# Two-layer hybrid decoder trunk on one core: the sums of the seven-product output projection move to VectorE, the planner's port rule changes, and the second layer's weight sums start earlier

## The chip, the cores and the metric

The kernel runs on one core of one Trainium2 chip. The metric is the device time of one execution in microseconds (us). The kernel before took 1146.99 us in the median of three runs (1146.76 to 1147.99). The execution that the profiler recorded took 1147.56 us; its instructions span 1145.8 us of that, so 1.8 us lie around the span. TensorE's granted clock was 0.996 of full speed over that span.

## The reference

Two layers follow each other; each maps x (1024 tokens of 1024 floats) to a new x. Cut to what matters:

```python
h = rmsnorm(x, g_pre) @ w_in                       # 1024 x 3488
(a_q, a_k, a_v, b_b, b_c, b_x, c_q, c_kv, c_kr, d_q, d_k, d_v, gate) = split(h)
ya = sliding-window attention with sinks           # group A, 256 columns
yb = b_b * (conv3(b_c * b_x) + conv_b)             # group B, 256 columns
yc = low-rank latent attention, causal             # group C, 256 columns
yd = stick-breaking attention, strictly causal     # group D, 256 columns
y = rmsnorm per group(ya, yb, yc, yd) * silu(gate) # 1024 x 1024
x = x + rmsnorm(y @ w_out, g_post)                 # y @ w_out: 1024 x 1024 x 1024
```

All of it is float32. The kernel keeps the operands of its large products as two parts, a high part and the rest ("hi" and "lo"), and forms each product as hi*hi + hi*lo + lo*hi. Such a pair of parts is called a split here: ScalarE writes hi (a cast), VectorE or GpSimd writes lo (source minus hi).

## The kernel before

**Stages of a layer.** First come the norm of the rows of x and their transposes (`prenorm_rows`, `prenorm_cols`), then the projections in the order of the stream `gemm()`: the columns of group C (`c_cols`, "projection one", which ends with the mark `("cn", l, 7)`), group B, then D, the gates and A. Attention scores (`scores`), the products with the values (`pvs`) and the group norms (`norms`) run between them. The last stage is y @ w_out.

**The seven products.** y and w_out are cut into two by two blocks of 512, and y @ w_out is formed with seven block products in place of eight (a Strassen-Winograd scheme). Product m (1 to 7) needs a left operand, a block or a sum of blocks of y (`left`, `y_sums1`, `y_sums2`, `difference`), and a right operand, a block or a sum of blocks of w_out. The right operands don't depend on x. The stream `weight_sums` forms them beforehand: for each of four row pairs k, `w_sums` loads two rows of blocks of w_out into two "P" tiles, and for each of the seven m forms a sum where there is one (four of the seven m), splits it (ScalarE casts hi, VectorE or GpSimd subtracts) and writes the split to DRAM scratch `rd[m][k]`. So each k has 4 sums and 7 splits, 11 VectorE-or-GpSimd instructions of 128x512; there are four k in each of two layers, 88 instructions in all. The stream `operands` later loads them again (`right`).

**The end of a layer.** The stream `outs` runs the products in the order 1, 7, 6, 4, 5, 2, 3, each for four token tiles i, combines them on VectorE, and calls `squares` (ScalarE squares with a row sum; VectorE scales; for the second half GpSimd takes the power -0.5). A gain multiplication by `norm_post` follows: for the first 512 columns in `outs`, for the second in `out_tile` (GpSimd in both places, except for the very last tile). `out_tile` then adds the normalised tile to x with two VectorE instructions, and in layer one starts the next layer's norm for that tile.

**What sets the order.** The class `Weaver` keeps a clock of its own for each engine (`busy`), with an estimated length for each instruction (`enter`). `place` looks for the first free spot of an engine; for instructions that read two SBUF operands or otherwise use the port that VectorE and GpSimd share (`pair`), it also looks at the other engine's list `port`. The planned time becomes the instruction's priority, and `behind` pins the order along each engine. TensorE's instructions stand in the order in which the streams issue them: `run` always advances the stream whose next step is ready first. `sooner` picks the engine, VectorE or GpSimd, on which one instruction would end first by that clock. Nothing of this clock runs on the chip; it only fixes which engine an instruction goes to and the order of each engine's queue. Six P tiles are shared by scores, norms and weight sums, counted in `ptiles`; "g" tiles (34) hold operands and "W" tiles (3) hold projection weights.

All VectorE, ScalarE and GpSimd instructions carry the line L85 in the profile, since `Tracked` issues them; matmuls are L513, transposes L517, DMA issues L430. So groups are told apart by the names of their tiles: xP are P tiles (rows of w_out, scores, rows of x), xg operand tiles, xw weight tiles or PSUM banks of projections, xraw raw weights, xtr, xsc and xpv other PSUM banks, xt scratch, xss the row sums of the output norm, xrd the DRAM scratch of the right operands.

## Time and profile before

| | |
|---|---|
| median of three runs | 1146.99 us |
| profiled execution | 1147.56 us |
| its span | 1145.8 us |
| TensorE (PE) busy | 1111.4 us, 97% |
| VectorE (DVE) busy | 853.6 us, 75% |
| ScalarE (ACT) busy | 683.4 us, 60% |
| GpSimd (POOL) busy | 437.4 us, 38% |
| DMA | 141.19 MB, mean 123 GB/s |

TensorE is busy nearly all the time, so what can be won is the time in which it waits, and the ends of the program, where it does not run. Those waits stand in a few stretches; the views by stretches and the timelines of single engines show them. In a timeline a line is one instruction or a run of equal ones: start, duration, engine, source line, operation, output<-inputs, count, and in brackets the idle time of the engine before it with what ended that. An instruction's duration covers its write at the end; the next one of the same engine starts somewhat before that, so the distance from start to start is a little shorter than the duration.

### The profile page before, as it was taken

What the parts mean: (1) busy time and instruction counts of PE and PEld (TensorE: products, weight loads), DVE (VectorE), ACT (ScalarE), POOL (GpSimd) and SP (SyncE); (2) the same over time, 40 slices, a digit from 0 to 9 for tenths busy, and PEclk for the clock granted to TensorE, in tenths of its full rate; (3) what the DMA queues carried; (4) which work ended last, traced back from release to release, by engine and by line L of the source; (5) the groups of instructions that cost most, each with busy time, mean ns of one, the idle gap of its engine ahead of it and who ended that gap; (6) DMA issues with size and microseconds to landing.
All of it is one profiled execution on the core that took longest, in us unless ns stands there. A gap on an engine that the chain in (4) does not pass through costs nothing.

```text
span 1145.8 us, 18194 instructions
## 1 busy us (share of the span) xinstructions
PE 1111.4 (97%) x6206; PEld 960.8 (84%) x6206; DVE 853.6 (75%) x1695; ACT 683.4 (60%) x1505; POOL 437.4 (38%) x542
## 2 busy tenths in 40 slices
PE   8999999899999999999989999999999999999996
PEld 6988888888888888788779888889888888887885
DVE  6868689868778758946785586898788885788376
ACT  7666567447767558634764655664677774773332
POOL 3216155423364216611631341453453631364034
PEclk9999999999999999999999999999999999999998
DMA  6120304842352023356550212068413411136544
GB/s 222 46 65 29 84 19 135 332 140 93 102 193 74 19 56 138 130 202 216 184 160 19 65 45 58 19 216 298 160 64 123 162 56 37 38 138 243 199 184 165
DMA packets 89887, 141.19 MB, mean 123 GB/s; under 512 B 12426, under 2 KB 61896, under 8 KB 89796
## 3 DMA queue, kind: packets, MB, share of 16 engines
q1 hardware_dynamic: 89796, 140.04, 37.0%
q8 instruction: 49, 0.80, 0.3%
q14 instruction: 42, 0.34, 0.1%
HBM read 88.64 MB, written 45.09 MB: 117 GB/s over the span
## 4 chain that ended last, share of the span: by engine, by line
PE 79%; DVE 9%; ACT 5%; issue 3%; POOL 3%; DMA 1%; SPq 0%; POOLq 0%; DVEq 0%; ACTq 0%
PE xw L513 47%; PE xsc L513 13%; PE xtr L517 9%; PE xpv L513 7%; DVE xg L85 4%; PE xtr L513 3%; ACT xP L85 3%; DVE xP L85 2%; ACT xg L85 1%; POOL xs L85 1%; DVE xPT L85 1%; DVE xs L85 1%; POOL xg L85 1%; DVE xt L85 0%; ACT xt L85 0%
## 5 line engine op out<-in xcount | busy, mean ns | idle before, releaser
L513 PE MATMUL xw<-xg,xw 128*128 128x512 f32 x2064 | 514.4, 396 | 1.4 <-DVE xg L85 1.4
L513 PEld LDWEIGHTS xw<-xg,xw 128*128 128x128 f32 x2064 | 377.0, 188 | 75.6 <-PE xsc L513 1.6
L513 PE MATMUL xsc<-xg,xg 128*128 128x512 f32 (+6 forms) x992 | 207.2, 350 | 1.0 <-issue 1.0
L513 PEld LDWEIGHTS xsc<-xg,xg 128*128 128x128 f32 (+1 forms) x992 | 161.0, 189 | 17.8 <-issue 1.4
L513 PE MATMUL xw<-xg,xg 128*128 128x256 f32 (+2 forms) x792 | 155.5, 343 | 0.9 <-DVE xg L85 0.9
L85 POOL TENSOR_SCALAR xP<-xP,xs 128x256 f32<-128x256 f32 (+7 forms) x128 | 80.2, 638 | 158.4 <-DVE xs L85 84.7
L513 PEld LDWEIGHTS xw<-xg,xg 128*128 128x128 f32 x792 | 130.2, 191 | 12.0 <-DVE xg L85 1.6
L517 PE MATMUL xtr<-ident,xP 128*128 128x128 f32 (+1 forms) x843 | 121.5, 273 | 7.6 <-DVE xg L85 5.7
L85 ACT CAST xPT<-xtr 128x512 fp32r<-128x512 f32 (+1 forms) x192 | 101.2, 558 | 45.8 <-PE xtr L517 44.3
L85 DVE TENSOR_TENSOR xPT<-xtr,xPT 128x512 fp32r<-128x512 f32 (+1 forms) x192 | 116.2, 628 | 14.3 <-ACT xPT L85 13.8
L513 PE MATMUL xpv<-xPT,xg 128*128 128x256 f32 (+1 forms) x720 | 115.8, 287 | 1.7 <-DVE xg L85 1.3
L513 PEld LDWEIGHTS xpv<-xPT,xg 128*128 128x128 f32 x720 | 103.2, 189 | 12.9 <-DVE xg L85 2.6
L517 PEld LDWEIGHTS xtr<-ident,xP 128*128 128x128 f32 (+1 forms) x843 | 96.9, 140 | 17.6 <-issue 9.9
L85 ACT ACTIVATE xP<-xP,xs 128x256 f32<-128x256 f32 (+7 forms) x132 | 85.0, 646 | 42.4 <-DVE xs L85 34.6
L85 DVE TENSOR_TENSOR_SCAN xP<-xP,xP 128x128 f32<-128x128 f32 (+3 forms) x64 | 90.7, 1427 | 13.6 <-ACT xP L85 12.7
L85 POOL TENSOR_TENSOR xw<-xraw,xw 128x512 fp32r<-128x512 f32 (+1 forms) x37 | 51.0, 1378 | 120.5 <-ACT xw L85 86.3
L85 DVE TENSOR_TENSOR xg<-xw,xg 64x512 fp32r<-64x512 f32 (+1 forms) x94 | 64.7, 688 | 36.9 <-ACT xg L85 33.1
L85 POOL TENSOR_TENSOR xg<-xg,xg 128x512 f32<-128x512 f32 (+1 forms) x33 | 44.5, 1355 | 118.5 <-ACT xt L85 100.0
L85 DVE TENSOR_TENSOR xg<-xg,xg 128x512 fp32r<-128x512 f32 (+3 forms) x80 | 63.0, 817 | 28.2 <-ACT xg L85 22.9
L85 ACT ACTIVATE xP<-xsc 128x512 f32<-128x512 f32 (+2 forms) x192 | 80.3, 517 | 2.9 <-PE xsc L513 2.4
L85 POOL TENSOR_TENSOR xs<-xs,mhalf 128x1 f32<-128x1 f32 (+2 forms) x36 | 35.9, 997 | 106.8 <-DVE xs L85 106.8
L85 ACT ACTIVATE xt<-xg 128x512 f32<-128x512 f32 (+1 forms) x88 | 46.4, 539 | 46.6 <-DVE xg L85 36.5
(137 smaller groups left out, 1519.8 us busy)
## 6 DMA issues: line engine op xcount, KB each, us to landing
xrd<-xg SPq DMA_DIRECT2D x56, 512.0 KB, 3.8
xg<-xrd SPq DMA_DIRECT2D x56, 512.0 KB, 5.3
xraw<-in_w_in_dram SPq DMA_DIRECT2D x96, 256.0 KB, 2.9
xP<-in_w_out_dram SPq DMA_DIRECT2D x16, 512.0 KB, 5.1
xg<-xyd SPq DMA_DIRECT2D x12, 512.0 KB, 4.2
xg<-in_x_dram SPq DMA_DIRECT2D x8, 512.0 KB, 9.6
xg<-xP SPq DMA_DIRECT2D x32, 128.0 KB, 2.3
xyd<-xg SPq DMA_DIRECT2D x8, 512.0 KB, 3.0
```

Source lines behind the costliest of these rows:

```text
L85: ins = real(*args, **kw)
L513: in_order(T.matmul(ps, lhs, rhs, start=start, stop=stop, skip_group_check=True))
L517: in_order(T.transpose(ps, src, idn))
```

## The change

Five things change.

1. `place`: the search for a spot now moves an instruction behind every entry of the other engine's port list that overlaps it (`s < t + dur and e > t`). Before, it moved it only where its start lay inside such an entry (`s <= t < e`).
2. `w_sums`: the sums and the splits are all VectorE instructions; `sooner` is not asked. 
3. `difference`, and the gain multiplications in `outs` and `out_tile`, are VectorE instructions.
4. `weight_sums` of the second layer may start when layer one's `outs` has started (`("u", l - 1)`), unless its rows are already being made ready (`calm`). Until projection one of its layer has ended, its splits go to a W tile, afterwards to a g tile. The first layer's waits only for `("cn", 0, 7)`. Both ask that VectorE be free within 900 ns by the clock (700 before).
5. In the list of streams `weight_sums` stands ahead of `outs`.

The matmuls are the same in number and shape. GpSimd loses 88 instructions (547 to 459 in its queue) and VectorE gains 88 (1697 to 1785). Of these a few are splits of projection weights (`w_split`), which `sooner` now gives to the other engine; two of them, of 128x416, stood in GpSimd's queue between the powers of the first row norms, in the program's first 20 us, and are VectorE's now.

```diff
@@ place
-            end = max([e for s, e in other if s <= t < e], default=t)
+            end = max([e for s, e in other if s < t + dur and e > t], default=t)
@@ w_sums
-            yield lambda: W.room("g", 1, 34) and not W.room("W", 1, 3) and max(0.0, free() - 700.0, W.ready("A", rows) - 1000.0)
+            early = lambda: ("cn", L["l"], 7) not in W.done
+
+            def where():
+                if early():
+                    return "W" if W.room("W", 1, 3) else None
+                return "g" if W.room("g", 1, 34) and not W.room("W", 1, 3) else None
+
+            yield lambda: bool(where()) and max(0.0, free() - 900.0, W.ready("A", rows) - 1000.0)
+            spot = where()
             if x1 is not None:
-                W.sooner((G, V), 512, x1, x2).tensor_tensor(dst, x1, x2, ALU.add)
-            t = gtile([P, 2, 512])
+                V.tensor_tensor(dst, x1, x2, ALU.add)
+            t = wtile() if spot == "W" else gtile([P, 2, 512])
             A.copy(t[:, 0, :], dst)
-            W.sooner((G, V), 512, dst, t).tensor_tensor(
-                t[:, 1, :], dst, f(t[:, 0, :]), ALU.subtract
-            )
+            V.tensor_tensor(t[:, 1, :], dst, f(t[:, 0, :]), ALU.subtract)
@@ difference
-        W.sooner((V, G), 512, x1, x2).tensor_tensor(dst, x1, x2, ALU.subtract)
+        V.tensor_tensor(dst, x1, x2, ALU.subtract)
@@ out_tile
-        (V if L["last"] and t == NT - 1 else G).tensor_tensor(u1, z, L["gpost"][:, 512:1024], ALU.mult)
+        V.tensor_tensor(u1, z, L["gpost"][:, 512:1024], ALU.mult)
@@ outs, twice
-                G.tensor_tensor(u21[i], u21[i], gain[:, 0:512], ALU.mult)
+                V.tensor_tensor(u21[i], u21[i], gain[:, 0:512], ALU.mult)
@@ weight_sums
-            yield need(("xt", l, 7), ("cn", l, 7))
+            yield need(("u", l - 1) if l else ("cn", l, 7))
             free = W.idle_from("V")
+
+            def calm():
+                rows = l and ("right", l - 1, 5, 0) in W.done and ("B", l) not in W.done
+                return not rows and ptiles[0] >= 3 and max(0.0, free() - 900.0)
+
             for k in range(4):
-                yield lambda: ptiles[0] >= 3 and max(0.0, free() - 700.0)
+                yield calm
```

**Place 1, GpSimd's queue in layer one, between two group norms.** Here xt and xg_1794 are the value products' last additions, xP_2528 and xP_2529 the two rows of w_out of `w_sums`, xw with xraw a split of projection weights, xs with mhalf the power of a group norm. Before:

```order
L85 TENSOR_TENSOR xt_2500<-xt_2500 64x128
L85 TENSOR_TENSOR xg_1794<-xt_2500 64x128
L85 TENSOR_TENSOR xP_2528<-xP_2528 128x512
L85 TENSOR_TENSOR xw_2557<-xraw_2403,xw_2557 128x512
L85 TENSOR_TENSOR xP_2528<-xP_2529,xP_2528 128x512
L85 TENSOR_TENSOR xs_2624<-xs_2624,mhalf 128x4
```

Of the change:

```order
L85 TENSOR_TENSOR xt_2500<-xt_2500 64x128
L85 TENSOR_TENSOR xg_1794<-xt_2500 64x128
L85 TENSOR_TENSOR xw_2552<-xraw_2403,xw_2552 128x512
L85 TENSOR_TENSOR xs_2632<-xs_2632,mhalf 128x4
L85 TENSOR_TENSOR xt_2643<-xt_2643 64x128
```

The two weight sums are gone from this queue; they now stand in VectorE's.

**Place 2, VectorE's queue at the boundary of the layers, between the additions of product 5 (from banks xsc and xpv) and the first one of product 2 (from a bank xw).** Additions from a bank set it free for TensorE. xP_59xx and xP_60xx with xss are the additions to x, xP_5889 and xP_5890 rows of w_out of the second layer. Before:

```order
L85 TENSOR_TENSOR xg_5882<-xsc_6155,xg_5882 128x512
L85 TENSOR_SCALAR xs_6116<-xs_6116 128x1
L85 SCALAR_TENSOR_TENSOR xP_5997<-xg_5959,xss_198,xP_5997 128x512
L85 SCALAR_TENSOR_TENSOR xP_5997<-xt_6138,xss_198,xP_5997 128x512
L85 TENSOR_TENSOR xg_5882<-xpv_6186,xg_5882 128x512
L85 TENSOR_SCALAR xs_6147<-xs_6147 128x1
L85 TENSOR_SCALAR xss_198<-xss_198 128x1
L85 TENSOR_TENSOR xg_5729<-xw_6248,xg_5729 128x512
```

Of the change:

```order
L85 SCALAR_TENSOR_TENSOR xP_6054<-xt_6195,xss_198,xP_6054 128x512
L85 TENSOR_TENSOR xg_5922<-xsc_6210,xg_5922 128x512
L85 TENSOR_TENSOR xg_5922<-xpv_6224,xg_5922 128x512
L85 TENSOR_TENSOR xw_6303<-xP_5889,xw_6303 128x512
L85 TENSOR_TENSOR xP_5889<-xP_5890,xP_5889 128x512
L85 TENSOR_TENSOR xg_5729<-xw_6256,xg_5729 128x512
L85 TENSOR_TENSOR xP_5890<-xP_5889,xP_5890 128x512
L85 TENSOR_SCALAR xss_198<-xss_198 128x1
L85 TENSOR_TENSOR xg_5729<-xg_5729,xg_5726 128x512
L85 TENSOR_TENSOR xg_5729<-xw_6274,xg_5729 128x512
```

The last two tiles of product 5 are added later, a split and a sum of the second layer's weights stand ahead of product 2's first addition, and a gain multiplication (by xg_5726) stands between its first and second.

**Place 3, VectorE's queue at the end of the program, product 3's tiles two and three.** Before:

```order
L85 TENSOR_TENSOR xg_11768<-xsc_12155,xg_11768 128x512
L85 TENSOR_SCALAR xss_231<-xss_231 128x1
L85 TENSOR_TENSOR xg_11769<-xsc_12180,xg_11769 128x512
L85 SCALAR_TENSOR_TENSOR xP_12228<-xg_11766,xss_231,xP_12228 128x512
L85 SCALAR_TENSOR_TENSOR xP_12228<-xt_12339,xss_231,xP_12228 128x512
L85 TENSOR_SCALAR xss_231<-xss_231 128x1
```

Of the change:

```order
L85 TENSOR_TENSOR xg_11768<-xsc_12155,xg_11768 128x512
L85 TENSOR_TENSOR xt_12339<-xg_11768,xg_11763 128x512
L85 TENSOR_SCALAR xss_231<-xss_231 128x1
L85 SCALAR_TENSOR_TENSOR xP_12228<-xg_11766,xss_231,xP_12228 128x512
L85 SCALAR_TENSOR_TENSOR xP_12228<-xt_12339,xss_231,xP_12228 128x512
L85 TENSOR_TENSOR xg_11769<-xsc_12180,xg_11769 128x512
L85 TENSOR_TENSOR xt_12363<-xg_11769,xg_11763 128x512
```

The gain multiplication (xt<-xg) joined the queue, and the third tile's addition from its bank moved behind the second tile's two additions to x.

Where the second layer's 28 splits are written out, by their place among TensorE's 6206 matmuls: before, 21 between the 4178th and the 4579th and 7 between the 4907th and the 4978th; now 13 between the 2783rd and the 3072nd (during layer one's seven products, which run from the 2775th to the 3126th), one at the 3500th, and 14 between the 4199th and the 4526th. One pair of P tiles stays with `w_sums` from the 2707th to the 3500th.

## Rows read from the trace of the kernel before

**Rows 1.** The page, part 1: busy time, share of the span, instructions.
```profile
PE 1111.4 (97%) x6206; PEld 960.8 (84%) x6206; DVE 853.6 (75%) x1695; ACT 683.4 (60%) x1505; POOL 437.4 (38%) x542
```

**Rows 2.** Stretches: us, busy (instructions) per engine, TensorE's clock, DMA share, GB/s.
```profile
0.00:20.00 20.00, 14.91 (x67) 10.37 (x68) 12.03 (x32) 14.07 (x35) 7.08 (x34) 1.00 0.92 315
196.00:262.00 66.00, 60.38 (x383) 54.94 (x382) 50.51 (x71) 33.70 (x63) 26.66 (x23) 0.97 0.67 240
458.00:500.00 42.00, 39.60 (x213) 32.44 (x212) 37.45 (x65) 22.01 (x48) 21.64 (x21) 1.00 0.45 159
540.00:602.00 62.00, 56.05 (x287) 47.10 (x286) 51.88 (x94) 41.71 (x99) 29.61 (x31) 1.00 0.56 181
760.00:830.00 70.00, 67.68 (x436) 61.11 (x434) 57.30 (x79) 39.31 (x74) 32.52 (x27) 1.00 0.68 239
1098.00:1146.00 48.00, 38.68 (x171) 31.72 (x169) 32.62 (x55) 14.45 (x38) 24.93 (x23) 0.93 0.45 167
```

**Rows 3.** Groups by shape, GpSimd: busy us, mean ns | idle before.
```profile
L85 POOL TENSOR_TENSOR xg<-xg,xg 128x512 f32<-128x512 f32 x32 | 43.4, 1363 | 118.4 <-ACT xt L85 100.0 <-DVE xg L85 18.1
L85 POOL TENSOR_TENSOR xg<-xP,xg 128x512 fp32r<-128x512 f32 x16 | 23.1, 1458 | 5.6 <-ACT xg L85 5.4
L85 POOL TENSOR_TENSOR xt<-xg,xg 128x512 f32<-128x512 f32 x15 | 21.4, 1428 | 2.5 <-DVE xg L85 2.3
L85 POOL TENSOR_TENSOR xP<-xP,xP 128x512 f32<-128x512 f32 x13 | 18.9, 1454 | 5.8 <-ACT xg L85 4.1 <-DVE xP L85 1.3
```

**Rows 4.** Groups by shape, VectorE.
```profile
L85 DVE TENSOR_TENSOR xg<-xP,xg 128x512 fp32r<-128x512 f32 x40 | 40.7, 1036 | 4.1 <-ACT xg L85 3.5
L85 DVE SCALAR_TENSOR_TENSOR xP<-xg,xss,xP 128x512 f32<-128x512 f32 x16 | 19.6, 1225 | 5.0 <-POOL xss L85 4.7
L85 DVE SCALAR_TENSOR_TENSOR xg<-xtr,xcols,xg 128x512 fp32r<-128x512 f32 x12 | 8.6, 745 | 8.6 <-ACT xg L85 8.6
```

**Rows 5.** Timeline of VectorE, 198 to 212 us: start, us, operation [idle before <-releaser].
```profile
199.01 4.68 DVE L85 TENSOR_TENSOR xg<-xP,xg 128x512 fp32r<-128x512 f32 x1
```

**Rows 6.** Timeline of GpSimd, 198 to 212 us.
```profile
198.56 0.85 POOL L85 TENSOR_TENSOR xg<-xt 64x128 f32<-64x128 f32 x1
...
201.87 1.28 POOL L85 TENSOR_TENSOR xP<-xP,xP 128x512 f32<-128x512 f32 x1
```

**Rows 7.** Timeline of TensorE, 198 to 212 us.
```profile
206.40 0.65 PE L517 MATMUL xtr<-ident,xt 128*128 128x128 f32 x4 [3.71 <-DVE xPT L85]
```

**Rows 8.** The stretch behind that wait.
```profile
206.80:211.40 4.60, 4.60 (x29) 4.60 (x28) 2.99 (x7) 2.81 (x6) 2.82 (x3) 0.63 0.84 305
```

**Rows 9.** Timeline of VectorE, layer two, 762 to 780 us.
```profile
767.78 2.15 DVE L85 TENSOR_TENSOR xg<-xP,xg 128x512 fp32r<-128x512 f32 x1
```

**Rows 10.** Timeline of VectorE, 0 to 20 us.
```profile
6.44 1.56 DVE L85 TENSOR_SCALAR xP<-xg,xs 128x1024 f32<-128x1024 f32 x1 [0.68 <-POOL xs L85]
...
19.34 0.75 DVE L85 TENSOR_SCALAR xP<-xg,xs 128x1024 f32<-128x1024 f32 x1 [0.66 <-POOL xs L85]
```

**Rows 11.** Timeline of VectorE, boundary of the layers, 538 to 602 us.
```profile
562.54 1.78 DVE L85 SCALAR_TENSOR_TENSOR xP<-xt,xss,xP 128x512 f32<-128x512 f32 x1
```

**Rows 12.** Timeline of VectorE, end of the program, 1126 to 1146 us.
```profile
1128.56 0.69 DVE L85 TENSOR_TENSOR xg<-xsc,xg 128x512 f32<-128x512 f32 x1 [0.50 <-PE xsc L513]
1130.11 0.21 DVE L85 TENSOR_SCALAR xss<-xss 128x1 f32<-128x1 f32 x1 [0.85 <-ACT xt L85]
1131.22 0.75 DVE L85 SCALAR_TENSOR_TENSOR xP<-xg,xss,xP 128x512 f32<-128x512 f32 x1 [0.91 <-POOL xss L85]
...
1132.56 0.68 DVE L85 TENSOR_TENSOR xg<-xsc,xg 128x512 f32<-128x512 f32 x1
...
1141.90 0.88 DVE L85 SCALAR_TENSOR_TENSOR xP<-xt,xss,xP 128x256 f32<-128x256 f32 x2
```

**Rows 13.** Timeline of TensorE, its last two lines.
```profile
1125.64 8.32 PE L513 MATMUL xsc<-xg,xg 128*128 128x512 f32 x36
1133.80 2.88 PE L513 MATMUL xpv<-xg,xg 128*128 128x512 f32 x12
```

More of the change, by code (lines that the diff above doesn't have):

```diff
@@ L1837, in outs @@
                 squares(L, 4 + i, 0, s1[i])
-                G.tensor_tensor(s1[i], s1[i], gain[:, 0:512], ALU.mult)
+                V.tensor_tensor(s1[i], s1[i], gain[:, 0:512], ALU.mult)
             for i in range(4):
@@ L2037, in tile_hybrid_trunk @@
         first_prenorm(), w_dma(tiles[8:]), w_split(tiles), norms(), next_prenorm(), pvs(), prep(), rope_tables(),
-        scores(), a_turn(), z_parts(), operands(), out_tiles(), outs(), weight_sums(), gemm(),
+        scores(), a_turn(), z_parts(), operands(), out_tiles(), weight_sums(), outs(), gemm(),
     ])
```

## The prediction, made before the changed kernel was run

> **What bounds the kernel now.** I read the page first. Part 1 gives TensorE 1111.4 us of busy time in a span of 1145.8 us [rows 1]: whatever the change does to the other engines, it can take away at most the 34.4 us in which TensorE is idle, apart from what the clock gives back. The table of stretches says where these lie [rows 2]: subtract PE's busy time from each stretch's length. The start has 5.09 us, layer one between its group norms (196 to 262) 5.62, its first products (458 to 500) 2.40, the boundary of the layers (540 to 602) 5.95, layer two's counterpart of the first place (760 to 830) 2.32, the end 9.32, of which 9.1 lie behind the last matmul (1133.80 + 2.88 = 1136.68 [rows 13], to 1145.8). That is 30.7 of 34.4.
>
> Then I read what holds TensorE there, in the timelines of single engines. At 206.40 it waits 3.71 us for VectorE [rows 7], and the clock granted behind that wait is 0.63 for 4.60 us [rows 8]: part of that stretch at 1.2 GHz, part at 2.4, a loss of 4.60 x 0.37 = 1.7 us more. VectorE is late because one addition of two SBUF operands lasts 4.68 us, from 199.01 to 203.69 [rows 5], where an addition of the same size whose second operand comes from a PSUM bank lasts 0.68 (at 1132.56 [rows 12]). Through all of it GpSimd works from instruction to instruction, from 198.56 to 203.15 [rows 6]; VectorE's addition ends half a microsecond behind the last of them. So a VectorE instruction with two SBUF operands can be held while GpSimd is busy. The same shows in means: 1036 ns for xg<-xP,xg and 1225 for xP<-xg,xss,xP, against 745 ns with an operand from a bank [rows 4].
>
> **The change part by part.** *Volume.* Four groups hold 76 of GpSimd's 88 instructions that leave: 43.4 + 23.1 + 21.4 + 18.9 = 106.8 us, 1.405 each [rows 3]; 88 x 1.405 = 124 us. On VectorE such an instruction costs 0.67 us from start to start (1131.22 to 1132.56 holds two [rows 12]), 88 x 0.67 = 59 us. Back come at least (1.036 - 0.68) x 40 = 14.3 and (1.225 - 0.745) x 16 = 7.7 us of holds. VectorE therefore goes from 853.6 to at most 853.6 + 59 - 22 = 891 us, 78% of the span; GpSimd to about 437 - 124 = 313. Over the whole span there is room; what counts is each stretch.
>
> *Layer one, 196 to 262.* The two weight sums leave GpSimd's queue (place 1); the split of a projection weight stays behind the value products' additions. The wait of 3.71 and the 1.7 of clock go. VectorE was 50.51 of 66 us busy [rows 2] and loses 4.0 us of hold, so six or seven moved instructions per row pair (at 0.67) fit. Best: all waits and the clock, -7.3. Worst: the remaining split holds VectorE twice by 1.47 us, as in the hold of 2.15 in rows 9 (2.15 - 0.68), leaving 5.4 - 2.9 = 2.5. I take -5.0, near the 5.4 that the rows tie to this one hold.
>
> *Layer two, 760 to 830.* Idle 2.32; one hold of 2.15 [rows 9] is worth 1.47. Fewer weight splits stand there now (7 of 28 less). From -2.3 to 0; I take -1.5.
>
> *Start.* A row's norm is held to 1.56 us against 0.75 free [rows 10], and TensorE's transposes wait for it, in two tiles. The two splits beside these norms are now VectorE's, behind the norm in its queue. From -2.8 to 0; I take -1.3, somewhat under 2 x 0.81.
>
> *The first products, 458 to 500 and the same place in layer two.* The differences move to VectorE: four in each, 2.7 us, while VectorE is 37.45 of 42 us busy, and the holds by GpSimd's differences go. The two cancel; from -2 to +3, I take 0.
>
> *The boundary, 540 to 602.* VectorE is 51.88 of 62 us busy, TensorE idle 5.95 in seven short waits for VectorE. About 12.5 gains (8.4 us) and five instructions for second-layer weights (3.4) move in: +11.8. What goes: seven instructions like that at 562.54, 1.78 us against 0.75 [rows 11, 12], 7 x 1.03 = 7.2, and some 1.5 of smaller holds. Net +3.1, 55 of 62 us. A gain of 1.4 us no longer stands in front of a norm's power in GpSimd's queue, and the chain of the next norm gets shorter by up to that. But place 2 shows a split and a sum ahead of product 2's first addition, which sets a bank free, and a gain between its first two: 0.67 each of new delay. Best: all 5.95 gone. Worst: half of the 11.8 ends up on TensorE's path, +6. I take -2.5, two of the seven waits' worth.
>
> *The early start of the second layer's sums.* 13 splits of 128 x 2 x 512 floats (0.52 MB, 6.8 MB in all) are written during layer one's products. DMA moves 159 to 181 GB/s there [rows 2], 305 in rows 8. I cost the transfers at nothing, with a bound of +6 (four right operands each late by one write, 0.52 MB at 305 GB/s = 1.7 us); nothing is gained where they leave except what stands above.
>
> *The end.* Per tile of product 3, VectorE now runs in one queue (place 3): addition to scaling 1.55 us, scaling to the additions to x 1.11, two additions 1.34 [rows 12], 4.0 us, and place 3 puts the next tile's bank addition behind that. TensorE needs 8.16 us for three tiles, 2.72 each [rows 13]. So VectorE falls behind. From 1128.56 I get the later bank additions at about 1133, 1137 and 1138.7 and the last addition to x ending at 1144.3, where it now ends at 1142.78 [rows 12]. From 0 (the holds that go pay for it) to +3; I take +1.5.
>
> *The port rule alone* moves instructions in the planned order only; its worth stands in the terms above.
>
> Sum: -5.0 - 1.5 - 1.3 + 0 - 2.5 + 0 + 1.5 = -8.8. Against the profiled execution, 1147.56 - 8.8 = 1138.8 us; that execution is 0.57 above the median, so 1138.2, told as 1138. The best ends sum to -20, the worst ones to +16 or so; they will not meet.
>
> **A rule against the row.** Rows 5 and 6 show one VectorE instruction waiting through four GpSimd instructions in a row. The Trainium skill, "SBUF — State Buffer", section "Who interferes with whom", says that the shared port pair is locked for one whole instruction by whoever issues first, that a VectorE instruction with two SBUF inputs contends with a GpSimd instruction that reads SBUF, and that one with at most one does not. Which operands collide agrees with the rows; by a lock of one instruction the hold would have ended at 199.41 (198.56 + 0.85), and it lasted 4.3 us longer. The row decides.
>
> **The rivals.** *A: the waits come back as VectorE's own queue.* Instead of being held, an addition stands behind a moved gain or sum. For it: 55 of 62 us at the boundary, the strict chain at the end. Against it: in 196 to 262 TensorE waits on a single long hold, not on a full queue. Then the boundary gives +2, the end +3, the first products +1, layer one only -4 and the rest -2: about 1147.
>
> *B: slower, VectorE sets the pace at the boundary.* In 540 to 602 some 21 moved instructions land, not 17 or 18, and the seven holds persist, because splits of projection weights and additions stay on GpSimd. Then VectorE needs 51.9 + 21 x 0.6 = 64.5 us for what now takes 62, and the fullest stretch that rows 2 show has it busy for 89% (37.45 of 42), with TensorE waiting there: 64.5 / 0.89 = 72.5, +10.5 on the path. With +3 at the end and the gains of the other three places (-7.8) that gives 1147 + 10.5 + 3 - 7.8 = 1153. It decides from the point at which VectorE's work there passes those 89%, 55 us; my own count comes just to it. For it: the earlier sums come into the same 60 us. Against it: the holds that I can name belong to gains, which leave. The Trainium skill, "Perfetto Trace Analysis", section "Optimizing Scalar/DVE Operations", speaks on this rival's side: where VectorE is saturated, giving some work to ScalarE or even GpSimd may make sense; it adds that between VectorE and GpSimd this might not help, as they share a port, and rows 5 bear out the addition.
>
> *C: the scratch writes delay the right operands.* The price is 4 to 6 us in layer one's products, the rest as forecast: about 1143. Against it: the DMA share there is 0.45 to 0.56 [rows 2].
>
> *D: the change doesn't do what it says.* The long hold doesn't come from GpSimd's run of instructions but ends with the first, and the 3.71 us have another cause that stays. Then layer one's term is 0 and half of the others' gain is left: about 1145. The lock's rule in the Trainium skill, taken alone, is this case. Against it: the ends at 203.69 and 203.15 [rows 5, 6].
>
> **How the numbers follow.** Forecast 0.58, by itself 1132 to 1144; A 0.18, B 0.13, C 0.06, D 0.05. A measurement of this kernel tells a change of 0.2%, 2.3 us, from none. Faster: nearly all of the forecast (0.57), C (0.05), a quarter of A (0.05), some of D (0.03): 0.70. Same: half of A (0.09) and pieces of the rest (0.05): 0.14. Slower: B (0.13) and some of A: 0.16. For 8 in 10 the range goes from 1130 (a term or two at their best) to 1149, into A and short of B.
>
> **What the next profile would show.** Right: VectorE 860 to 890 us, GpSimd near 315; xP<-xg,xss,xP down from 1225 to about 800 ns, xg<-xP,xg from 1036 to about 720; no wait over 2 us for the transposes of layer one's group norms and a clock of 1.00 behind them; under 4 us of idle TensorE at the boundary; some 10.5 us behind the last matmul. Wrong: more idle TensorE at the boundary than 6 us with bank additions of VectorE as releasers (A, B); waits of layer one's products for a DMA (C); an instruction of VectorE still over 3 us long beside GpSimd's splits (D).

## The result and the profile after

The changed kernel took 1131.02 us (median of four runs, 1129.0 to 1131.47) against 1146.88 (1146.16 to 1147.99), a ratio of 0.9857 with a 95% interval of 0.984 to 0.9875: 15.9 us faster. The forecast was 1138, with a range of 1130 to 1149; the measured time lies 1 us inside the range and just below the 1132 to 1144 that the prediction gave to its own forecast. The profiled execution took 1130.98 us, its span is 1129.2.

Part 1 of the page answers to [rows 1]:

```profile
PE 1110.1 (98%) x6206; PEld 963.3 (85%) x6206; DVE 869.8 (77%) x1783; ACT 684.3 (61%) x1505; POOL 312.4 (28%) x454
```

GpSimd lost 125 us of work and VectorE gained only 16, though 88 instructions moved. The moved instructions cost some 59 us by the prediction's 0.67 us each, so about 43 us came back. The groups show part of it (to be set beside [rows 4]): instructions of the same two kinds take 749 and 750 ns where they took 1036 and 1225, which is 11.5 us over the 40 of before and 7.6 over the 16.

```profile
L85 DVE TENSOR_TENSOR xg<-xP,xg 128x512 fp32r<-128x512 f32 x43 | 31.3, 749 | 5.6 <-ACT xg L85 5.4
L85 DVE SCALAR_TENSOR_TENSOR xP<-xg,xss,xP 128x512 f32<-128x512 f32 x16 | 12.0, 750 | 4.0 <-POOL xss L85 3.7
```

The stretches, with the columns of [rows 2] (work that lies late in the program comes up to 16 us earlier now, so the last ones hold somewhat later work):

```profile
0.00:20.00 20.00, 16.59 (x72) 11.70 (x73) 11.61 (x35) 14.87 (x36) 5.49 (x33) 1.00 0.91 315
196.00:262.00 66.00, 65.87 (x419) 59.08 (x418) 56.84 (x88) 37.91 (x76) 16.39 (x15) 1.00 0.70 248
458.00:500.00 42.00, 41.92 (x223) 35.70 (x222) 34.22 (x53) 17.79 (x32) 4.20 (x3) 1.00 0.60 231
540.00:602.00 62.00, 56.49 (x288) 49.78 (x288) 48.57 (x102) 42.45 (x102) 16.04 (x19) 0.94 0.47 161
760.00:830.00 70.00, 70.00 (x439) 62.38 (x437) 52.77 (x83) 37.84 (x76) 17.88 (x16) 1.00 0.46 158
```

TensorE is idle for 0.13, 0.08 and 0.00 us where it was idle for 5.62, 2.40 and 2.32. At the boundary 5.51 are left, where the prediction had under 4, now with a clock of 0.94.

A better measure goes by TensorE's matmuls: each kernel runs 6206, so the time from the n-th matmul to a later one can be compared. Below is the difference to before, in us, for each kernel of this study (an edit of one part in the upper rows). Each row is one profiled execution. In the last two rows the order of the matmuls is that of before, and cells far from the edit still differ by up to 1.4 us. In the other rows matmuls also change places across a bound, which moves time between neighbouring cells. An estimate that gives each kind of matmul its median spacing changes cells before 535 by at most 0.5 us and cells behind it by up to 2.9, most where two neighbours differ in sign; the sum of such neighbours is safer than either.

| kernel | start to 186 | norms, layer one (186-262) | 262-440 | first products (440-520) | boundary (535-610) | 610-735 | norms, layer two (735-840) | 840-1000 | first products (1000-1056) | 1056-1136 | end |
|---|---|---|---|---|---|---|---|---|---|---|---|
| the change | -1.4 | -7.2 | +1.0 | -3.4 | +1.9 | -0.9 | -3.9 | +0.1 | -2.2 | -0.7 | 0.0 |
| port rule alone | +0.3 | -5.7 | +0.3 | -0.3 | -1.2 | -0.5 | -0.3 | 0.0 | -0.5 | -0.3 | +1.4 |
| sums alone | -0.1 | -7.8 | +1.7 | +0.1 | 0.0 | -0.7 | -1.8 | -0.5 | 0.0 | 0.0 | 0.0 |
| differences alone | +0.2 | 0.0 | 0.0 | -2.9 | 0.0 | -0.4 | 0.0 | 0.0 | -2.3 | -0.2 | 0.0 |
| gains alone | +0.1 | -0.2 | 0.0 | +0.1 | -1.6 | -0.7 | +0.1 | 0.0 | -0.1 | 0.0 | 0.0 |
| change, sums not early | -1.4 | -7.2 | +3.5 | -2.8 | -3.3 | -0.5 | -2.4 | +2.9 | -3.8 | -0.6 | 0.0 |
| change, old port rule | +0.3 | -7.4 | +0.4 | -3.0 | +1.6 | -0.9 | -1.1 | +0.1 | -2.2 | -0.2 | 0.0 |
| change, gains on GpSimd | -1.6 | -7.2 | +1.0 | -3.4 | +4.2 | -0.3 | -0.3 | 0.0 | -2.2 | -0.7 | +1.4 |
| change, sums wait | -1.1 | -7.2 | +1.0 | -3.4 | -0.1 | +0.4 | -3.7 | -1.2 | -2.2 | -0.7 | 0.0 |
| the same, four banks for product 2 | -1.2 | -7.2 | +1.0 | -3.3 | -0.1 | +1.8 | +3.2 | -0.8 | -2.2 | -0.7 | 0.0 |
| sums wait, product 3 later | -0.9 | -7.2 | +1.0 | -3.5 | -2.2 | +1.5 | +3.1 | -1.3 | -2.2 | -0.7 | +1.9 |
| before, one more on GpSimd (scratch) | +0.2 | +1.1 | 0.0 | +0.1 | 0.0 | -0.7 | 0.0 | 0.0 | -0.1 | 0.0 | 0.0 |
| before, one more on GpSimd (in place) | +1.4 | -3.0 | 0.0 | +0.1 | +0.1 | -0.2 | 0.0 | 0.0 | +0.1 | 0.0 | 0.0 |

(The bounds are the times of before; 520 to 535 is 0.0 in all.)

**Layer one's norms.** The weight sums are gone from GpSimd's queue, the transposes come without a wait and the clock stays at 1.00 ([rows 5 to 8] before). VectorE, GpSimd and TensorE of the change, each by its timeline:

```profile
203.79 0.69 DVE L85 TENSOR_TENSOR xg<-xP,xg 128x512 fp32r<-128x512 f32 x1
```
```profile
196.56 0.46 POOL L85 TENSOR_TENSOR xg<-xt 64x128 f32<-64x128 f32 x1
198.13 1.37 POOL L85 TENSOR_TENSOR xw<-xraw,xw 128x512 fp32r<-128x512 f32 x1 [1.11 <-ACT xw L85]
```
```profile
202.05 0.63 PE L517 MATMUL xtr<-ident,xt 128*128 128x128 f32 x4
```

**The boundary.** The one long wait of the changed kernel is here. TensorE's timeline, and the stretch behind the wait:

```profile
528.71 8.32 PE L513 MATMUL xsc<-xg,xg 128*128 128x512 f32 x36
536.87 2.88 PE L513 MATMUL xpv<-xg,xg 128*128 128x512 f32 x12
539.59 5.60 PE L513 MATMUL xw<-xg,xg 128*128 128x512 f32 x24
548.77 6.45 PE L513 MATMUL xw<-xg,xg 128*128 128x512 f32 x15 [3.59 <-DVE xg L85]
```
```profile
548.80:555.00 6.20, 6.20 (x15) 4.87 (x16) 3.38 (x8) 3.54 (x7) 0.54 (x1) 0.52 0.32 108
```

Product 5's four tiles go to the banks xsc and xpv, product 2's first two to the two banks xw; the third waits 3.59 us for the addition that sets the first free. Behind it the clock is 0.52 for 6.20 us, nearly all of it at 1.2 GHz: 6.2 x 0.48 = 3.0 us more. VectorE's queue shows why the addition is late:

```profile
538.40 0.69 DVE L85 TENSOR_TENSOR xg<-xg,xg 128x512 fp32r<-128x512 f32 x1 [1.36 <-ACT xg L85]
539.01 0.68 DVE L85 TENSOR_TENSOR xg<-xsc,xg 128x512 f32<-128x512 f32 x1
...
546.83 0.69 DVE L85 TENSOR_TENSOR xw<-xP,xw 128x512 fp32r<-128x512 f32 x1
547.43 0.69 DVE L85 TENSOR_TENSOR xP<-xP,xP 128x512 f32<-128x512 f32 x1
548.03 0.69 DVE L85 TENSOR_TENSOR xg<-xw,xg 128x512 f32<-128x512 f32 x1
```
```profile
537.74 0.62 ACT L85 CAST xg<-xg 128x512 fp32r<-128x512 f32 x1 [1.49 <-PE xpv L513]
```

Product 2's first tile was done at 539.59 + 2.72 = 542.3; its addition comes 5.7 us later. The weight split and sum ahead of it are 1.2 of these. The rest comes from further ahead in the queue: product 5's first tile was done at 528.71 + 2.72 = 531.4 and is added at 539.01, 7.6 us later. In the kernel before, this addition came 1.4 us behind its tile (539.66 + 2.72 = 542.38, then 543.78), so the late queue is new. TensorE and VectorE of before:

```profile
539.66 8.32 PE L513 MATMUL xsc<-xg,xg 128*128 128x512 f32 x36
```
```profile
543.78 0.68 DVE L85 TENSOR_TENSOR xg<-xsc,xg 128x512 f32<-128x512 f32 x1
```

In the changed kernel a split of a left operand stands in front of the addition, at 538.40; its cast on ScalarE waits for TensorE's reading in product 5's last tile (537.74). From there on VectorE works with hardly a pause.

**The end.** The spacing of the bank additions is 3.74 us, much as worked out, and 9.1 us lie behind the last matmul, as before [rows 12, 13]:

```profile
1111.97 0.69 DVE L85 TENSOR_TENSOR xg<-xsc,xg 128x512 f32<-128x512 f32 x1 [0.48 <-PE xsc L513]
...
1115.71 0.69 DVE L85 TENSOR_TENSOR xg<-xsc,xg 128x512 f32<-128x512 f32 x1
...
1125.33 0.87 DVE L85 SCALAR_TENSOR_TENSOR xP<-xt,xss,xP 128x256 f32<-128x256 f32 x2
```

### The profile page after: what moved, and what is told of

Same layout as the page of the kernel before. It is cut to its first block, busy times and chain, and to the rows that moved or that the text cites. A ratio compares the mean times of both kernels' runs of the same rounds, so it can differ in the third digit from the quotient of the medians.

```text
span 1129.2 us, 18118 instructions
## 1 busy us (share of the span) xinstructions
PE 1110.1 (98%) x6206; PEld 963.3 (85%) x6206; DVE 869.8 (77%) x1783; ACT 684.3 (61%) x1505; POOL 312.4 (28%) x454
## 4 chain that ended last, share of the span: by engine, by line
PE 90%; ACT 4%; DVE 3%; issue 1%; POOL 1%; DMA 0%; POOLq 0%; DVEq 0%; ACTq 0%
PE xw L513 53%; PE xsc L513 15%; PE xtr L517 10%; PE xpv L513 8%; PE xtr L513 3%; ACT xP L85 2%; DVE xg L85 1%; ACT xg L85 1%; DVE xP L85 1%; ACT xt L85 1%; PE xtr L594 0%; PE xsc L517 0%; DVE xs L85 0%; DVE xPT L85 0%; DVE xf L85 0%
## 5 line engine op out<-in xcount | busy, mean ns | idle before, releaser
L85 POOL TENSOR_SCALAR xP<-xP,xs 128x256 f32<-128x256 f32 (+7 forms) x128 | 77.2, 613 | 170.7 <-DVE xs L85 85.6
L85 DVE TENSOR_TENSOR_SCAN xP<-xP,xP 128x128 f32<-128x128 f32 (+3 forms) x64 | 88.2, 1392 | 6.7 <-ACT xP L85 5.8
L85 DVE TENSOR_TENSOR xg<-xg,xg 128x512 fp32r<-128x512 f32 (+3 forms) x113 | 80.4, 747 | 15.8 <-ACT xg L85 12.2
L85 POOL TENSOR_TENSOR xt<-xt 64x128 f32<-64x128 f32 x64 | 47.3, 739 | 149.1 <-DVE xt L85 118.2
L85 POOL TENSOR_TENSOR xw<-xraw,xw 128x512 fp32r<-128x512 f32 (+1 forms) x34 | 46.2, 1358 | 143.7 <-ACT xw L85 97.5
L85 ACT CAST xw<-xraw 128x512 fp32r<-128x512 f32 (+1 forms) x91 | 56.3, 621 | 31.0 <-PE xw L513 25.6
```

What stands on the lines that cost most here:

```text
L85: ins = real(*args, **kw)
```

## The experiments

The theory: VectorE's instructions with two SBUF operands are held while GpSimd works, TensorE waits for them, and the change wins by taking GpSimd's work away. The rivals: it is the new order of the queues, or the waits only change their cause.

**One part at a time.** The port rule alone (the one line in `place`):

> The kernel before with the new port rule of the ordering clock and nothing else. GpSimd still has 421 of its instructions in its queue (444 before, 369 in the change). Theory: what costs is that GpSimd's instructions hold VectorE's on the chip, and a planned order alone removes only part of it: in layer one between the group norms a value product's last addition, a weight split and a copy still follow each other on GpSimd, so a hold of some 2 to 3.5 us of one addition stays (4.68 before). Wait at the first group norm's transposes 1 to 2.5 us (3.71 before), first products about as before. Total 1141 to 1146. Rival (the order of the queues is what counts, not the engine that does the work): waits at the norms and in the first products mostly gone, 1136 or less.

1141.28 us, ratio 0.9945 (0.9923 to 0.9966). The total is within the theory's range, but at the norms the rival was right: the theory left a wait of 1 to 2.5 us at the transposes, and none is left. Most of the gain, 5.7 us, lies there, where the new order stretches GpSimd's instructions apart. So order counts too, as it decides what overlaps.

The sums and splits alone:

```diff
-                W.sooner((G, V), 512, x1, x2).tensor_tensor(dst, x1, x2, ALU.add)
+                V.tensor_tensor(dst, x1, x2, ALU.add)
-            W.sooner((G, V), 512, dst, t).tensor_tensor(
+            V.tensor_tensor(
```

> The kernel before with the sums and splits of w_out's blocks on VectorE alone; the port rule, the differences, the gains and the start of the second layer's sums stay as before. Theory (holds): the wait of 3.71 us at the first group norm of layer one and the clock's fall behind it go, and layer two's wait of 1.8 at its counterpart; idle of TensorE in these two stretches from 7.9 to under 2 us; 1.7 us of clock come back. First products (458 to 500, and in layer two) and the boundary keep their waits. Total 1147 minus 8 to 10: 1137 to 1139. Rival (VectorE's own queue takes the place of the holds): the wait at the transposes keeps over 2 us, now behind sums, and the total is 1144 or more.

1138.74 us, ratio 0.9924 (0.9908 to 0.9941). In its stretches TensorE waits no more at either layer's norms, while the boundary keeps its 6 us:

```profile
196.00:262.00 66.00, 66.00 (x424) 59.26 (x423) 48.85 (x81) 35.46 (x71) 16.02 (x15) 1.00 0.53 188
540.00:602.00 62.00, 55.99 (x292) 48.10 (x291) 48.07 (x91) 41.28 (x102) 28.18 (x31) 1.00 0.47 146
```

VectorE is less busy there (48.85 us, 50.51 before) with more to do. The rival of the queue falls for this place.

The differences alone (`V.tensor_tensor` in `difference`):

> The kernel before with the differences of blocks of y on VectorE alone. GpSimd's queue around the first layer's group norms is the one of before, so the wait of 3.71 us there must stay (a control). Theory (holds): in the first products of either layer the additions and differences that last 1.2 to 1.6 us beside GpSimd's differences fall to 0.7, and the waits of 1.2 to 1.4 us for the next scores' transposes there go: 2 to 4 us in each layer, total 1139 to 1143. Rival (that VectorE has no room there: it was 37.45 of 42 us busy, and four more instructions cost what the holds cost; the forecast's term of 0): total 1145 to 1148, the waits as long.

1142.23 us, ratio 0.9956 (0.9942 to 0.9971). The control holds (its first stretch below has 60.40 us busy, as before), and the first products gain 2.9 and 2.3 us, though VectorE is 40.01 us busy there (458 to 500), more than before:

```profile
196.00:262.00 66.00, 60.40 (x384) 54.93 (x383) 50.95 (x71) 33.53 (x63) 26.46 (x23) 0.97 0.67 239
458.00:500.00 42.00, 41.69 (x225) 35.04 (x224) 40.01 (x72) 22.54 (x49) 11.57 (x13) 1.00 0.48 159
```

What went is a wait for the next transposes behind two held additions (3.34 us for two), VectorE and TensorE of before; with the differences on VectorE TensorE waits at most 0.2 us for one thing between 440 and 520.

```profile
467.96 3.34 DVE L85 TENSOR_TENSOR xg<-xg,xg 128x512 fp32r<-128x512 f32 x2
```
```profile
472.10 0.63 PE L517 MATMUL xtr<-ident,xP 128*128 128x128 f32 x4 [1.19 <-DVE xg L85]
```

The gains alone (`V` for `G` in `outs` and `out_tile`):

> The kernel before with the gain multiplications of the output norm on VectorE alone; no second-layer sums stand near the boundary of the layers. Theory (holds, and the early sums are what is late there in the change): the held additions to x of 1.77 us fall to 0.75, the idle time of TensorE in the boundary falls from 5.95 to 2 to 4 us with no single wait over 2 us and a clock of 1.00; the end of the program stays within 1 us of 9.1 behind the last matmul. Total 1142 to 1145. Rival (the gains themselves fill VectorE's queue ahead of product 2's first additions, as in the change): one wait of 3 us or more about the start of product 2 with a clock below 1.00 behind it, total 1146 to 1150.

1145.16 us, ratio 0.9978 (0.9968 to 0.9987). No single wait over 2 us at the boundary and a clock of 1.00; 1.6 us gained there, nothing at the end. The gains in VectorE's queue are not what makes the change's long wait. The idle time, 4.75 us, stayed above the 2 to 4 expected, and the total lies just above the theory's 1142 to 1145.

```profile
540.00:602.00 62.00, 57.25 (x296) 48.81 (x295) 50.73 (x103) 42.49 (x103) 19.32 (x23) 1.00 0.56 181
```

The four gains add up to 23.9 us of spans, the change has 16.6: the port rule and the sums cure the same place (5.7 and 7.8 of 7.2), and the boundary gets worse when all is together.

**One part less.** Without the early start (parts 4 and 5 of the change undone):

> The change without its parts 4 and 5: the second layer's sums wait for the end of its own projection one, as before, and all stand on VectorE. Theory (the wait of 3.59 us and the 1.2 GHz stretch about the start of product 2 come from the early sums, which put VectorE's queue behind by their split and sum and by what is planned around them): no single wait over 2 us at the boundary, clock 1.00, idle of TensorE there 3 to 5 us, layer two between its norms still without waits, as in the kernel with the sums alone; total 1125 to 1128, 3 to 6 us under the change. Rival (the early start pays, since it takes 14 splits out of a full stretch of layer two): waits of 2 us or more come back behind layer two's norms, total 1132 or more.

1132.21 us, ratio 0.9871 (0.9856 to 0.9886). The theory was right on the place and wrong on the sum: at the boundary the wait is down to 1.67 us, the clock stays at 1.00 and 5.2 us are gained against the change. Product 5's first addition comes 2.1 us behind its tile here. It is 1.4 to 2.1 us in every kernel of this study without the early start, and 4.1 to 8.9 in every one with it, so the late queue comes with the early start. But 2.5 us are lost from 262 to 440 and 1.5 at layer two's norms; of the 2.8 from 840 to 1000, 1.6 come back in the next cell. The total is the rival's, without a wait of 2 us behind layer two's norms. So the early start costs at the boundary and seems to pay elsewhere, though the two kernels' totals aren't told apart by their intervals; which of the moved splits pay was not traced, and parts 4 and 5 were not tried apart.

```profile
550.82 5.83 PE L513 MATMUL xw<-xg,xg 128*128 128x512 f32 x24 [1.67 <-DVE xg L85]
```

With the old port rule:

> The change with the old port rule. Theory (holds by the moved instructions are the main cause): the first layer's norms and the first products stay free of waits; lost are the start (two splits of projection weights beside the first norms, 1 us) and some holds by projection-weight splits, 1 to 3 us in all: 1131 to 1134. Rival (the rule itself brings its 6 us that it brought alone): 1136 or more.

1135.18 us, ratio 0.9892 (0.9876 to 0.9909), between the two expectations: the rule is worth about 4 us within the change, 1.7 of them at the start and 2.8 at layer two's norms, where splits of projection weights still run on GpSimd. That those splits make the 2.8 is not shown (see layer two's norms under the repairs).

With the gains back on GpSimd:

> The change with the gain multiplications back on GpSimd. Theory (the gains' holds at the boundary cost about what their place in VectorE's queue costs; alone their move brought 2.4 us): holds of 1.77 us return at the boundary and the end, the idle of TensorE at the boundary stays at 5 to 7 us; total 1131 to 1135. Rival (the wait of 3.59 us in the change comes from the gains in VectorE's queue): that wait is gone and the total is 1128 or less.

1138.53 us, ratio 0.9924 (0.9909 to 0.9939): 7.5 us slower than the change, more than either expectation. The held additions return and the long wait stays; its rival falls. Of the 7.5 us, 2.3 lie at the boundary and 1.4 at the end, where the gains run; 3.6 lie at layer two's norms, which the edit doesn't touch. VectorE and TensorE of this kernel:

```profile
541.34 1.76 DVE L85 SCALAR_TENSOR_TENSOR xP<-xg,xss,xP 128x512 f32<-128x512 f32 x1 [0.44 <-POOL xss L85]
```
```profile
548.66 6.71 PE L513 MATMUL xw<-xg,xg 128*128 128x512 f32 x21 [3.72 <-DVE xg L85]
```

**The hold by itself.** An instruction was added to GpSimd's queue of before, behind the sum into `b` of the first row pair:

```diff
+                if (L["l"], k, m) == (0, 0, 5):
+                    junk = ttile([P, 512])
+                    nc.gpsimd.tensor_tensor(junk, dst, dst, ALU.add)
```

> The kernel before with one instruction more on GpSimd: a sum of two 128x512 operands into scratch that nobody reads, in its queue right behind the second weight sum that stands behind the first value products' additions in layer one (the four instructions in a row across which VectorE's addition lasted 4.68 us). All else in both queues stays. Theory (the addition is held as long as GpSimd goes from instruction to instruction without a gap): it lasts 4.68 + 1.25 = 5.9 us, TensorE's wait at the group norm's transposes grows from 3.71 to about 5.0, and the clock falls again behind it. Rival (the hold covers one instruction of GpSimd, or a fixed time, and the rest of the 4.68 has another cause): the addition stays at 4.7 us, the wait at 3.7. Total 1148 to 1149 or 1147.

A miss: the scratch tile came free late, so the instruction began 2.68 us behind the row (205.94) and the hold was 4.64 us. It tells neither way. VectorE and GpSimd of this kernel:

```profile
199.16 4.64 DVE L85 TENSOR_TENSOR xg<-xP,xg 128x512 fp32r<-128x512 f32 x1
```
```profile
205.94 1.04 POOL L1583 TENSOR_TENSOR xt<-xP 128x512 f32<-128x512 f32 x1 [2.68 <-DVE xt L85]
```

The second try multiplies in place and waits for nothing but the sum before it:

```diff
+                    nc.gpsimd.tensor_scalar(dst, dst, 1.0, 0.0, ALU.mult, ALU.add)
```

> The kernel before with one instruction more on GpSimd that needs nothing that isn't there yet: the sum that stands first of the three 128x512 instructions behind the first value product's last addition in layer one is followed by a multiplication of its result by 1, in place (128x512). In the kernel hold_longer the added instruction had to wait for its scratch tile, came after the row, and so told nothing. All else in the queues of VectorE, ScalarE and GpSimd stays. Theory (VectorE's addition is held as long as GpSimd goes from instruction to instruction without a gap): it lasts longer by the whole of the added instruction, 0.5 to 1.3 us, to 5.2 to 6.0 us, and TensorE's wait at the transposes grows by the same, from 3.71 to 4.2 to 5.0. Rival (the hold is one instruction's, or fixed): the addition stays at 4.7 us, the wait at 3.7.

Neither came true: the hold got shorter. VectorE, GpSimd and TensorE of this kernel:

```profile
200.37 2.19 DVE L85 TENSOR_TENSOR xg<-xP,xg 128x512 fp32r<-128x512 f32 x1
...
203.69 0.69 DVE L85 TENSOR_TENSOR xf<-xw,xf 128x512 f32<-128x512 f32 x1
204.29 0.98 DVE L85 TENSOR_TENSOR xt<-xt,xt 128x512 f32<-128x512 f32 x1
```
```profile
199.93 0.84 POOL L85 TENSOR_TENSOR xg<-xt 64x128 f32<-64x128 f32 x1
200.73 1.28 POOL L85 TENSOR_TENSOR xP<-xP 128x512 f32<-128x512 f32 x1
202.10 0.94 POOL L1581 TENSOR_SCALAR xP<-xP 128x512 f32<-128x512 f32 x1
203.02 1.71 POOL L85 TENSOR_TENSOR xw<-xraw,xw 128x512 fp32r<-128x512 f32 x1
204.68 1.72 POOL L85 TENSOR_TENSOR xP<-xP,xP 128x512 f32<-128x512 f32 x1
```
```profile
205.93 0.66 PE L517 MATMUL xtr<-ident,xt 128*128 128x128 f32 x4 [1.88 <-DVE xPT L85]
```
```profile
206.30:211.00 4.70, 4.70 (x42) 4.70 (x41) 3.97 (x9) 2.89 (x6) 2.93 (x4) 1.00 0.97 319
```

The first two of GpSimd's instructions overlap by 0.04 us, and VectorE is held through both. The added one needs the result of the one before it and starts 0.09 us after its end (200.73 + 1.28 = 202.01 to 202.10). VectorE gets in there, and its addition ends at 202.56. TensorE waits 1.88 us in place of 3.71 and keeps its clock; the stretch of layer one's norms is 3.0 us shorter, with one instruction more. The single time, 1145.94, is too little for a verdict, but the place shows that GpSimd's row sets the length of the hold, and the hold TensorE's wait.

It doesn't show that only a gap lets VectorE in. In the same rows VectorE's addition at 204.29 ends at 205.27, 0.54 us behind GpSimd's split (203.02 + 1.71 = 204.73), though GpSimd's next record begins 0.05 us before that end; now it is this next one that lasts longer, 1.72 us. In the kernel before, ten more joins of two 128x512 instructions of GpSimd have records that overlap and a VectorE instruction with two SBUF operands that waits. At each of the ten this instruction ends 0.55 us behind GpSimd's first, after 0.99 to 1.65 us in all, and GpSimd's second takes 1.72 to 1.75 us in place of 1.28. One of them, VectorE and GpSimd:

```profile
544.38 1.22 DVE L85 TENSOR_TENSOR xg<-xg,xg 128x512 fp32r<-128x512 f32 x1
```
```profile
543.75 1.30 POOL L85 TENSOR_TENSOR xg<-xg,xg 128x512 f32<-128x512 f32 x1 [3.79 <-ACT xt L85]
545.00 1.74 POOL L85 TENSOR_TENSOR xt<-xg,xg 128x512 f32<-128x512 f32 x1
```

Of VectorE's 128x512 instructions with two SBUF operands, only those at two places are held on past such a join: this one and the one of [rows 9], in each of the five kernels that have them. In both the hold begins in GpSimd's 64x128 addition xg<-xt. So the usual hold lasts for the rest of one GpSimd instruction; why it goes on at these two places stays open, and whether the gap, the dependence or the other kind of instruction ended it in this kernel was not told apart.

**Repairs of the boundary.** The sums wait there step by step as well:

```diff
+            held = lambda: l and ("right", l - 1, 5, 0) in W.done and ("B", l) not in W.done
-            yield lambda: bool(where()) and max(
+            yield lambda: not held() and bool(where()) and max(
```

> The change, but a step of the second layer's sums also waits while the boundary runs (from the loading of product 5's right operands until group B's projection), as the start of a new row pair already does; so the split and the sum that stand ahead of product 2's first addition go elsewhere. Theory: that addition comes 1.2 us or more earlier, the wait of 3.59 us falls to 2.4 or less and its 1.2 GHz stretch gets shorter or goes; total 1126 to 1130. Rival (the wait has its length from the additions to x and of product 5 planned ahead of it, not from the two): the wait stays over 3 us, total within 1 us of the change.

1129.57 us, ratio 0.9841 (0.9827 to 0.9856), the fastest measured; its interval overlaps the change's, so it is not shown to be better. At the boundary 2.0 us come back, and the wait is 2.38 as expected:

```profile
547.85 5.28 PE L513 MATMUL xw<-xg,xg 128*128 128x512 f32 x15 [2.38 <-DVE xg L85]
```

Then, on top of it, two more banks for product 2, `("w", "tr")` in both layers:

> The kernel in which the sums also wait while the boundary runs, and product 2 may in layer one, as it may in layer two, also take the two banks that the transposes use. Theory (TensorE stands still there because product 2's third tile needs the bank of its first, whose addition is late in VectorE's queue; with four banks the queue has two tiles' time, 5.4 us, more): the wait of 2.38 us at product 2 and the 1.2 GHz behind it go; part of it comes back since the next norm's transposes must wait for those banks. Total 1124 to 1128. Rival (the transposes' wait takes its place in full): 1129 to 1132.

1137.86 us, ratio 0.9918 (0.9902 to 0.9935), above both expectations. The wait for the bank goes and returns at the transposes (1.22 and 1.47 us below), which was the rival's mechanism; the boundary stands where it did (-0.1 against before). Of the 8.3 us that are lost against the base, 6.9 are at layer two's norms (+3.2 against before, where the base has -3.7).

```profile
550.04 0.30 PE L517 MATMUL xtr<-ident,xP 128*128 128x128 f32 x1 [1.22 <-DVE xs L85]
551.81 0.55 PE L517 MATMUL xtr<-ident,xP 128*128 128x128 f32 x3 [1.47 <-ACT xP L85]
```

Last, the operands of product 3 only after product 5's additions are in the queues:

```diff
+                    elif m == 3:
+                        yield need(("halves", l, 3))
                     elif m in (5, 2, 3):
```

> The kernel in which the sums also wait while the boundary runs, and the operands of product 3 are made only after product 5's additions are in the queues (they were free to start with those of products 5 and 2). In the change VectorE stands 1.36 us, and in the kernel it starts from 2.34 us, ahead of product 5's first addition at a split of a left operand, whose cast on ScalarE waits for a tile that product 5 reads last; the addition, whose bank was full at about 531.5 us, comes at 539. Theory (this late queue, not the number of moved instructions, is what TensorE waits for at product 2): product 5's additions come 5 us or more earlier, the wait at product 2 goes, and the time is 1123 to 1127. Rival (product 3's operands are then late themselves): a wait at product 3 of 2 us or more, total 1129 or more.

1136.89 us, ratio 0.9909 (0.9892 to 0.9925); the theory had 1123 to 1127, and the rival's wait at product 3 isn't what costs. At its place it does what was expected in part: product 5's first addition comes at 535.94 (539.29 in its base, so 3.4 us earlier where 5 were expected), TensorE waits 0.58 us at product 2, the clock stays at 1.00, and the boundary has -2.2 us. But layer two's norms again lose 6.8 us against the base, and the end 1.9. The largest wait of TensorE there:

```profile
744.02 0.63 PE L517 MATMUL xtr<-ident,xt 128*128 128x128 f32 x4 [3.19 <-DVE xt L85]
```

No edit touches that place. Its queues come out in another order, since the planner goes on from another clock. VectorE also has more to do between the same two matmuls of TensorE there: 86.14 us with four banks and 86.50 here, 80.62 in their base. Whether that makes the loss is not shown, and why this order is the slower one stays open, as does the question whether a version with both gains can be had.

## Why the prediction was right, and where not

**The main mechanism was right.** VectorE 869.8 and GpSimd 312.4 us (forecast 860 to 890, near 315), the two means at 750 and 749 ns (800, 720), no wait at layer one's norms, clock 1.00. Two of its signs missed: 5.51 us of idle TensorE at the boundary (under 4), 9.1 behind the last matmul (10.5). Rival B fell: the boundary is VectorE-late, but for 1.9 us, not 10.5, with VectorE 48.57 of 62 us busy. Rival A came true at the boundary alone, and nowhere else. Rival C fell: no DMA stands among the releasers of TensorE's waits. Rival D fell, since the wait of 3.71 us went with the weight sums (no wait at these transposes in the kernel with the sums alone) and fell to 1.88 where the hold was cut to 2.19.

The Trainium skill, "SBUF — State Buffer", section "Who interferes with whom", was weighed beforehand: its lock is held for one whole instruction. The runs agree with it on the operands (the addition fed from a bank at 203.69 takes 0.69 us in the middle of GpSimd's 1.71) and, at the ten joins above, on the length. They differ at two places: 4.68 us through four instructions, 2.15 through two [rows 5, 9]. There the measurement decides. The prediction took the exception, one row of four instructions, for the rule; that did no harm, as the one long hold was what its largest term rested on. By GpSimd's own ends that hold passed the first instruction by 3.7 us (199.41 to 203.15); the prediction's 4.3 counts to the end of VectorE's addition. The Trainium skill, "Perfetto Trace Analysis", section "Optimizing Scalar/DVE Operations", says that giving VectorE's work to GpSimd might not help, since they share a port. The runs agree: the gains given back to GpSimd cost 2.3 us at the boundary and 1.4 at the end.

**The sizes, term by term.** The forecast's -8.8 became -16.6 in the spans. That the range held is in part luck: the boundary came out 4.4 us worse than forecast, and without that the time would have been about 1126.6, under the range's 1130 (an estimate: 1131.0 - 4.4).

- *Layer one's norms:* -5.0 forecast, -7.2 measured, the best end of the range. The remaining split on GpSimd now stands alone (198.13, 1.37 us); no wait of TensorE follows from it, where the range's worst end had it hold VectorE twice.
- *The first products:* 0 forecast, -3.4 and -2.2 measured. This is the term that failed most: "The two cancel" weighed 2.7 us of moved differences against the holds by VectorE's busy time. The kernel with the differences alone shows VectorE busier (40.01 against 37.45) and TensorE's idle time down from 2.40 to 0.31. What counted was that the held additions stood ahead of the next transposes (467.96 and 472.10 above); the busy share said nothing on that.
- *Layer two's norms:* -1.5 forecast, -3.9 measured; the sums alone bring 1.8. Without the port rule it is -1.1, without the early start -2.4; but edits that don't touch this place leave anything from -3.7 to +3.2 there, so the rest is not shown to be theirs.
- *The boundary:* -2.5 forecast, +1.9 measured, on the other side but within the bounds. The delay of 0.67 us each for a split and a sum was right; that the early start would make the queue in front of them 7.6 us late (1.4 before), behind a split that waits for TensorE itself, was not seen. The prediction's seven held additions there were six of 1.76 to 1.78 us and one of 1.23, so 6.6 us and not 7.2. The order alone, read at place 2, can't show it: only the trace has the times at which each instruction's inputs come.
- *The start:* -1.3 forecast, -1.4 measured, up to 186 us.
- *The end:* +1.5 forecast, 0.0 measured. The chain came out at 3.74 us a tile, but before it was already 4.0 from the first addition to the second [rows 12]; with the gains on GpSimd the end is 1.4 us longer, so the holds there cost at least what the longer queue costs.
- *The scratch writes:* no cost to TensorE.

The forecast fell 7.8 us short of the gain in the spans: 5.6 at the first products, 2.2 and 2.4 at the norms, 1.5 at the end, against 4.4 too much at the boundary; what remains lies in the stretches that had no term.

## What to carry to other kernels

Where GpSimd runs instruction after instruction, look at VectorE's longest instructions with two SBUF operands first: their excess over the mean of a bank-fed one is a stall of an in-order queue, and what TensorE waits for may stand behind it. Judge a move by which instruction is late for TensorE, not by the busy share of the engine that takes it. And with a planner behind the order, compare traces matmul by matmul: a repair in one place can lose more in a place that it doesn't touch.

## What the runs showed that was not expected

- One VectorE addition was held through four GpSimd instructions, 4.68 us; one dependent instruction more in the row made it 2.19. At ten other joins of GpSimd's instructions, no wider, VectorE got in after the first.
- In the four kernels whose queue at layer one's norms is that of before, or all but that (before, differences alone, gains alone, one more on GpSimd with scratch), the hold is 4.64 to 4.70 us long: it is no chance event.
- Behind TensorE's wait of 3.59 us the granted clock was 0.52 for 6.2 us; with the wait of 3.71 in before it was 0.63 for 4.6; behind a wait of 3.70 in the kernel with one more on GpSimd (scratch) it was 0.50 for 4.6, and behind the wait of 1.88 in the one that multiplies in place it was 1.00.
- Layer two's norms took from 3.9 us less to 3.2 us more than before, in kernels whose edits against each other lie elsewhere.
